# Moving the substitution rounds of a DeltaNet layer behind weight splits and the scaling of the last keys

## The chip, the cores and the metric

The kernel runs on one core of a Trainium2 chip, as one launch. The metric is the device time of an execution in microseconds (us); less is better. The core has five engines, each with an instruction queue of its own that is worked off in order: TensorE (PE in the profile; its weight loads are PEld), VectorE (DVE), ScalarE (ACT), GpSimd (POOL), and SyncE (SP), which here only issues transfers. ScalarE also issues some transfers of weights.

## The reference

One layer of a hybrid diffusion backbone, on 1024 latent tokens and 256 context tokens, width 1024, all in float32. A normalised and modulated input goes through one projection into two branches:

```python
h = rmsnorm(x, g_pre) * (1.0 + scale[:, None]) + shift[:, None]
na_q, na_k, na_v, na_z, g_qkv, g_z, g_b, g_a = jnp.split(h @ w_in, IN_SPLITS, axis=-1)
o_na = neighborhood_attention(...)            # 8 heads of 64, 8 x 16 window on a 16 x 64 grid, plus context keys
q, k, v = gdn_qkv(g_qkv, conv_w)              # 5-tap conv, SiLU, l2norm of q and k; 4 heads of 128
q, k = axial_rope(q, rope), axial_rope(k, rope)
beta, g = gdn_gates(g_b, g_a, A_log, dt_bias)
o_g, o_gc = bidirectional_gdn(q, k, v, g, beta, qc, kc, vc, gc, betac)
o_g = rmsnorm(o_g, gdn_norm_w)
y = jnp.concatenate([o_na * jax.nn.silu(na_z), o_g * jax.nn.silu(g_z)], axis=-1) @ w_out
x = x + gate[:, None] * rmsnorm(y, g_post)
```

The second branch is a gated delta rule in chunks, in both directions. Each chunk needs the inverse of a unit triangular matrix (`triangular_solve`), and `l2norm` divides queries and keys by the root of a sum of squares.

## The kernel before

Products are made from two halves: each operand is split into a high half (`hi`, rounded on ScalarE) and a low half (`lo`, the rest), and three matmuls (hi hi, hi lo, lo hi) add up in PSUM, so each weight goes through L585 (high half, ScalarE) and L586 (low half, GpSimd or VectorE) in `load_w` before TensorE can use it. The raw weights have three buffers; the transfer of a later weight, issued on ScalarE's queue (L582), waits until a raw buffer has been split.

Phase 0 normalises and modulates the inputs. Phase 2 runs over the four DeltaNet heads h. For each head, a string of letters gives the order in which the steps are emitted: Q, K, V (`conv`: projection and convolution), R (`res_gate`), T (`qk_tok`), B (`qk_back`), U (the values' transposes), p (the next part of `projections`, work for TensorE from the attention branch and the gates), and F (`delta_front`, the products of the head's keys and queries, emitted once the next head's Q and K are). In the last head the p's are a key projection of the attention (`na_proj`), the two halves of a gate (`gate_proj`, L704 its last instruction on VectorE), and the first two tiles of `values`, for which the weight `nv0` is loaded in four pieces (k0 = 0, 2, 4, 6; `wr_nv`, `wh_nv` and `wl_nv` in the profile).

`qk_tok` transposes queries (`which` = 1) and keys (`which` = 0) to token order, takes the sums of squares on ScalarE (L1068), takes the keys' root on GpSimd (`rsqrt`, L218 and L219), scales the keys by it on VectorE (L1074) and rotates both: L1084 and L1085 are the products with sine and cosine, L1086 the sum. The queries' rotation is on GpSimd, the keys' on VectorE, and both share two buffers `rot` (tag `sr`). The queries are not scaled here; their roots (`rho`, L218 and L219 on 32 columns) are taken in `delta_load` and used in the scan. `qk_back` transposes back (L1097, `tb`) and stores. `delta_front` follows with `pk` (PE), `pm` and `qe` (VectorE, L1189 and L1192), stores them, and copies `pm` from memory to memory (L1200, `ab_dram`).

`inv_pairs` inverts the 32 x 32 diagonal blocks of the first heads, two groups of 120 blocks side by side, one block a partition, in 30 substitution rounds from m = 30 down to 1; a round is a product (L1233) and a sum (L1235) on VectorE over 2 m (31 - m) elements. It starts in the last head: it yields after the load and after every even m, and the loop over the letters advances it by one yield per letter. At its end the blocks are stored (L1241, `yd`). In phase a2, which runs the rest of the projections (`na_proj` of pairs 2 and 3 among them), `inv_merge` loads the blocks (L1285, `vl`), transposes them on VectorE (L1291 to L1293, `vx`, `vd`, `ld`) and merges them into the chunk's inverse with small products (L1305 the first, `tz`). Then come attention and scan together (phase b) and the output projection (phase 4).

The order of each engine's queue is fixed when the kernel is built, by a list scheduler that keeps a time line of its own estimates: of what is ready there, it takes what was emitted first (`tc.high_priority` lets the merges count as emitted earlier). `self.order(r, name)` adds to it that instruction r stands behind another one; for two instructions of one engine this is an order on the queue and no wait.

Of the kernel before, what the change touches and what calls it, by code (L numbers as in the profile page):

```python
# [11 lines left out]
F32 = mybir.dt.float32  # L12
# [8 lines left out]
P = 128  # L21
# [110 lines left out]
def bc(ap, shape):  # L132
    return ap.to_broadcast(shape)
# [57 lines left out]
class K:  # L191
# [21 lines left out]
            self.nc.sync.dma_start(self.dbg[name], ap)  # L213


    def rsqrt(self, pool, x, n, tag, eps):
        y = pool.tile([P, n], F32, name=f"rq_y_{tag}", tag=f"rq_y{n}")
        self.nc.gpsimd.tensor_scalar(y, x, eps, None, ALU.add)  # L218
        self.nc.gpsimd.tensor_tensor(y, y, bc(self.mhalf, [P, n]), ALU.pow)  # L219
        return y  # L220


# [347 lines left out]
    def load_w(self, pool, c0, n, tag, bufs=(3, 4, 4), halves=2, load=None, ks=None, dst=None, later=None):  # L570


        nc = self.nc
        kk = len(ks) if ks else KC // halves
        his, los = [], []
        for k0 in [ks[0]] if ks else range(0, KC, kk):
            wt = lambda c, dt, nb: pool.tile([P, 528], dt, name=f"w{c}_{tag}_{k0}", tag=f"w{c}", bufs=nb)[
                :, :kk * n].rearrange("p (k n) -> p k n", k=kk)
            raw = wt("r", F32, bufs[0])
            hi, lo = dst or (wt("h", F32R, bufs[1]), wt("l", F32R, bufs[2]))  # L580
            src = self.I["w_in"]
            (load or nc.scalar.dma_start)(raw.rearrange("p k n -> p (k n)"), bass.AP(  # L582
                src.tensor, W_OFF[tuple(c0) if isinstance(c0, list) else ((c0, n),)] + k0 * n, [[KC * n, P], [1, kk * n]]))
            if later is None:
                nc.scalar.copy(hi, raw)  # L585
                (nc.vector if halves > 2 and k0 % 4 else nc.gpsimd).tensor_tensor(lo, raw, hi.bitcast(F32), ALU.subtract)  # L586
            else:
                later.append(lambda c, hi=hi, lo=lo, raw=raw: nc.scalar.copy(hi, raw) if c == "h" else
                             nc.vector.tensor_tensor(lo, raw, hi.bitcast(F32), ALU.subtract))
            for j in range(kk):  # L590
                his.append(hi[:, j, :])
                los.append(lo[:, j, :])
        return his, los
# [102 lines left out]
    def gate_proj(self, ap, ps, j, c0, w=None):  # L696
        nc = self.nc
        w = w or self.load_w(self.wp, c0, P, f"gz{j}")
        for gr in range(2):
            pz = ps.tile([P, 512], F32, name=f"pz{j}_{gr}", tag="pj", bufs=3)  # L700
            self.mm_chan(pz, w, self.hh, self.hl, 512 * gr, 512)
            z = self.wp.tile([P, 512], F32, name=f"st_z{j}{gr}", tag="st", bufs=4)
            nc.scalar.activation(z, pz, AF.Tanh, scale=0.5)
            nc.vector.scalar_tensor_tensor(z, z, 1.0, pz, ALU.add, ALU.mult)  # L704
            nc.sync.dma_start(self.z_dram[P * j:P * j + P, 512 * gr:512 * gr + 512], z)
            yield

# [239 lines left out]
    def phase2(self):  # L947
        tc, nc, I = self.tc, self.nc, self.I
        ps = self.ps
        with tc.tile_pool(name="cv", bufs=1, side="right", reuse_waits="tile") as cv:  # L950
# [37 lines left out]
            for h in range(4):  # L988
                for c in "QK":
                    step(h, c)  # L990
                    next(blocks, None)
                for _ in blocks:
                    pass
                step(h - 1, "F") if h else step(h, "G")
                if h == 3:
                    blocks = self.inv_pairs(cv)
                for c in ("RVpppTUpB", "RppVTpUBp", "RVTpUpB", "VRppTppUB")[h]:
                    step(h, c)
                    next(blocks, None)
            step(3, "F")  # L1000
            for _ in blocks:
                pass
# [47 lines left out]

    def qk_tok(self, cv, ps, h, qa, ka, rope):
        nc, col = self.nc, self.col
        toks = []
        for which, acc in ((1, qa), (0, ka)):
            groups = ((2, 4), (6, 4)) if which else ((0, 2), (2, 4), (6, 4))
            first, m = groups[0][0], 10 - 2 * which
# [2 lines left out]
            for t0, n in groups:  # L1059
# [9 lines left out]
                                         accum_out=ss[:, t0 + t - first:t0 + t - first + 1])  # L1069
                pts.append((t0, n, pt, tok))  # L1070
            r = None if which else self.rsqrt(cv, ss, m, f"g{h}", 4 * EPS)
            for t0, n, pt, tok in pts:
                if not which:
                    nc.vector.tensor_tensor(tok[:, :n, :], pt[:, :n, :],  # L1074
                                            bc(r[:, t0 - first:t0 - first + n].unsqueeze(2), [P, n, P]), ALU.mult)
                if t0:
                    rot = cv.tile([P, 4, P], F32, name=f"rot{h}_{which}{t0}", tag="sr", bufs=2)
                    x5, r5 = (v.rearrange("p t (a s c) -> p (t a) s c", a=2, s=2) for v in (tok, rot))

                    xs = bass.AP(tok.tensor, tok[:, 0, 32:].offset, [list(tok.ap[0]), [64, 8], [-32, 2], [1, 32]])  # L1080
                    cs = rope[:, 64 * (t0 - 2):64 * (t0 + 2)].rearrange("p (b c) -> p b c", c=32)
                    sn = rope[:, 512 + P * (t0 - 2):512 + P * (t0 + 2)].rearrange("p (b s c) -> p b s c", s=2, c=32)
                    eng = nc.gpsimd if which else nc.vector
                    eng.tensor_tensor(r5, xs, sn, ALU.mult)  # L1084
                    eng.tensor_tensor(x5, x5, bc(cs.unsqueeze(2), [P, 8, 2, 32]), ALU.mult)  # L1085
                    eng.tensor_tensor(tok, tok, rot, ALU.add)  # L1086
                toks.append((which, t0, n, tok))
        return toks

# [130 lines left out]
    def inv_pairs(self, pool):  # L1220
        nc = self.nc
        ab = pool.tile([P, 2 * S], F32, name="ab", tag="ab")
        tb = pool.tile([P, 480], F32, name="tb", tag="tb")[:120]
        for g in range(2):
            w = self.inv_load(g, ab[:, S * g:S * g + S])
            nc.gpsimd.affine_select(w, w, [[-1, 32], [1, 32]], ALU.is_gt, 0.0, base=0, channel_multiplier=0)
        ab = ab[:120].rearrange("p (g a b) -> p g a b", g=2, a=32)
        nc.gpsimd.memset(bass.AP(ab.tensor, ab.offset, [list(ab.ap[0]), [S, 2], [33, 32]]), 1.0)
        yield
        for m in range(30, 0, -1):  # L1230
            n = 31 - m
            t3 = tb[:, :2 * m * n].rearrange("p (g a b) -> p g a b", g=2, a=m)
            nc.vector.tensor_tensor(t3, bc(ab[:, :, 0:m, m:m + 1], [120, 2, m, n]), bc(ab[:, :, m:m + 1, m + 1:], [120, 2, m, n]),  # L1233
                                    ALU.mult)
            nc.vector.tensor_tensor(ab[:, :, 0:m, m + 1:], ab[:, :, 0:m, m + 1:], t3, ALU.add)  # L1235
            if m % 2 == 0:
                yield
        yield
        for g in range(2):
            self.yd[g] = self.dp.tile([120, 32, 32], F32, name=f"yd{g}")  # L1240
            nc.sync.dma_start(self.yd[g], ab[:, g])  # L1241
# [112 lines left out]
    def delta_load(self, g3, h):  # L1354
# [10 lines left out]
        if h == 0:  # L1365
# [1 line left out]
            nc.vector.tensor_scalar(fl(self.nsc), fl(self.egc), -1.0, None, ALU.mult)  # L1367
            nc.vector.tensor_tensor(self.nsc[:, :, 1, :], self.nsc[:, :, 1, :], self.beta[:, :, 1, :], ALU.mult)

            self.rho = self.rsqrt(self.cp, self.ssq.rearrange("p h t -> p (h t)"), 32, "rho", 4 * EPS)  # L1370
            self.rho2 = self.cp.tile([P, 32], F32, name="rho2")
            nc.gpsimd.tensor_tensor(self.rho2, self.rho, self.rho, ALU.mult)
        return kq, v, kt_, *(w.rearrange("p (d t) c -> p d t c", d=2) for w in (tm, qe))
# [390 lines left out]
```

## Time and profile before

| what | value |
|---|---|
| time, median of 3 runs | 853.98 us (848.8 to 854.83) |
| the profiled execution's own time | 848.82 us |
| its span, first to last instruction | 847.1 us |
| TensorE busy | 814.2 us, 96% |
| VectorE, ScalarE, GpSimd busy | 495.0, 418.0, 365.5 us |
| granted TensorE clock, mean | 0.99 |

Lines of a timeline give start, duration, engine, source line, operation, output and input, count, and in brackets the idle time of the engine before it with what ended it. Lines of waits give who waited for whom, the total, the number of times and the longest. L586 is line 586 of the kernel before.

### The profile page before, as it was taken

Reading aid. Unit: us, or ns where it says so; the run is one execution under the profiler, and the core shown is the slowest. Engines: PE = TensorE matmul, PEld = TensorE weight load, DVE = VectorE, ACT = ScalarE, POOL = GpSimd, SP = SyncE. Lnnn points to the kernel's source line nnn. Section 1 sums busy time; section 2 is a strip of 40 time slices with the busy share of each in tenths; the row PEclk is TensorE's granted clock in tenths of the full one; section 3 lists DMA queues with packets and bytes.
Section 4 is the critical chain, followed back from the end, with each engine's and each line's share of the span. In section 5 each row is a group of like instructions: output and inputs, shape, how many; then the busy total and the mean of one; then the engine's idle time right before and its main releaser. Section 6 shows DMA issues by size and latency. Waiting matters only on the chain.

```text
span 847.1 us, 16613 instructions
## 1 busy us (share of the span) xinstructions
PE 814.2 (96%) x6170; PEld 695.3 (82%) x6170; DVE 495.0 (58%) x988; ACT 418.0 (49%) x1097; POOL 365.5 (43%) x436
## 2 busy tenths in 40 slices
PE   8999999999999999988997999899999999999996
PEld 6688887888788878878985787799898989878885
DVE  4673455546456757699926955556566565743342
ACT  4472525654564664643214334566666666753211
POOL 0042221363482572555452103565757567835121
PEclk9999999999999999999998999999999999999999
DMA  9986442254626626733688579996967923234261
GB/s 332 341 305 213 136 138 90 79 180 161 162 75 227 197 69 230 218 110 102 202 241 239 166 223 293 392 306 181 313 186 257 250 97 128 87 125 137 99 199 50
DMA packets 86343, 159.67 MB, mean 188 GB/s; under 512 B 18405, under 2 KB 45750, under 8 KB 84086
## 3 DMA queue, kind: packets, MB, share of 16 engines
q1 hardware_dynamic: 78774, 144.94, 54.0%
q10 hardware_dynamic: 7488, 13.67, 5.5%
q8 instruction: 49, 0.80, 0.4%
q14 instruction: 32, 0.26, 0.1%
HBM read 109.51 MB, written 52.42 MB: 191 GB/s over the span
## 4 chain that ended last, share of the span: by engine, by line
PE 76%; DMA 9%; DVE 7%; POOL 3%; issue 2%; ACT 2%; SPq 0%; DVEq 0%; POOLq 0%; ACTq 0%
PE py L1550 4%; PE py L1552 3%; PE py L1551 3%; PE pz L607 3%; PE pz L608 3%; PE pz L603 3%; PE pa L1437 3%; DMA vl<-yd 2%; PE po L942 2%; PE po L937 2%; PE tr L926 2%; PE sc L905 2%; PE pa L1422 2%; PE pv L618 2%; PE pv L617 2%; PE pv L616 2%
## 5 line engine op out<-in xcount | busy, mean ns | idle before, releaser
L909 DVE CUSTOM_DVE_ANT_0 pt<-sc,gm 128x544 f32<-128x544 f32 (+1 forms) x64 | 49.4, 772 | 32.3 <-PE sc L905 28.6
L910 ACT ACTIVATE pt<-pt,nm 128x544 f32<-128x544 f32 (+1 forms) x64 | 50.5, 789 | 31.1 <-DVE nm L909 30.7
L893 POOL TENSOR_TENSOR gm<-gt,mk 128x288 f32<-128x288 f32 (+1 forms) x48 | 46.5, 972 | 21.8 <-DVE nm L909 18.6
L1412 POOL TENSOR_SCALAR kd<-kt,kd 128x128 f32<-128x128 f32 x72 | 42.7, 604 | 18.7 <-PE pa L1451 18.2
L1040 DVE SCALAR_TENSOR_TENSOR acc_v<-xp_v,cols,acc_v 128x1282 f32<-128x1282 f32 x16 | 33.1, 2068 | 26.9 <-ACT acc_v L1038 26.6
L1193 POOL TENSOR_SCALAR_AFFINE_SELECT qe<-qe 128x256 f32<-128x256 f32 x32 | 29.0, 907 | 39.8 <-DVE qe L1192 39.8
L1616 DVE TENSOR_TENSOR finv<-py,ggb 128x512 f32<-128x512 f32 (+1 forms) x17 | 10.7, 656 | 51.4 <-ACT finv L1615 43.0
L603 PE MATMUL pz<-hh,wh_gz 128*128 128x512 f32 x96 | 38.9, 405 | 0.0
L607 PE MATMUL pz<-hl,wh_gz 128*128 128x512 f32 x96 | 38.8, 405 | 0.0
L608 PE MATMUL pz<-hh,wl_gz 128*128 128x512 f32 x96 | 38.8, 404 | 0.0
L1174 ACT ACTIVATE em<-em,gc 128x128 f32<-128x128 f32 x80 | 25.5, 390 | 25.7 <-DMA em<-gc_dram 22.9
L618 PE MATMUL pv<-wl_nv,hh 128*128 128x264 f32 x104 | 30.5, 296 | 4.8 <-DVE wl_nv L586 4.8
L1189 DVE SCALAR_TENSOR_TENSOR pm<-pk,nsc,em 128x128 f32<-128x128 f32 x80 | 23.5, 342 | 18.5 <-PE pk L1182 14.6
L1418 POOL TENSOR_SCALAR vb<-v,beta 128x128 f32<-128x128 f32 x40 | 24.2, 606 | 23.0 <-DVE y L1424 13.1
L586 POOL TENSOR_TENSOR wl_gz<-wr_gz,wh_gz 128x512 fp32r<-128x512 f32 x12 | 15.5, 1290 | 37.3 <-ACT wh_gz L585 35.8
L926 PE MATMUL tr<-c,pt 128*96 128x128 f32 (+1 forms) x192 | 31.4, 273 | 0.0
L1454 DVE SCALAR_TENSOR_TENSOR s<-s,egl,pa 128x128 f32<-128x128 f32 x64 | 19.4, 342 | 20.1 <-PE pa L1451 20.1
L924 ACT COPY tcx<-tc 128x256 f32<-128x256 f32 x64 | 23.5, 367 | 15.1 <-PE tc L919 14.5
L928 ACT COPY tl<-tr 96x384 f32<-96x384 f32 (+1 forms) x64 | 30.5, 476 | 0.0
L617 PE MATMUL pv<-wh_nv,hl 128*128 128x264 f32 x104 | 30.0, 291 | 0.0
L616 PE MATMUL pv<-wh_nv,hh 128*128 128x264 f32 x104 | 29.2, 292 | 0.0
L1615 ACT ACTIVATE finv<-py 128x512 f32<-128x512 f32 x14 | 8.3, 598 | 38.7 <-PE py L1552 20.5
(469 smaller groups left out, 2859.3 us busy)
## 6 DMA issues: line engine op xcount, KB each, us to landing
wada<-in_w_ada SPq DMA_DIRECT2D x16, 512.0 KB
em<-gc_dram SPq DMA_DIRECT2D x20, 256.0 KB
pm_dram<-pm SPq DMA_DIRECT2D x20, 256.0 KB
tm_dram<-tm SPq DMA_DIRECT2D x8, 640.0 KB
kk<-qk_dram SPq DMA_DIRECT2D x16, 320.0 KB
tm<-tm_dram SPq DMA_DIRECT2D x4, 1280.0 KB
kq_dram<-kq SPq DMA_DIRECT2D x4, 1152.0 KB
kq<-kq_dram SPq DMA_DIRECT2D x4, 1152.0 KB
```

The costliest lines, as they stand in the source:

```text
L603: r = nc.tensor.matmul(ps, wh, xh, start=(k == 0 and first), stop=False)
L607: nc.tensor.matmul(ps, wh, xl, start=False, stop=False)
L608: nc.tensor.matmul(ps, wl, xh, start=False, stop=(k == KC - 1))
L616: nc.tensor.matmul(ps, xh, wh, start=(k == 0), stop=False)
L617: nc.tensor.matmul(ps, xl, wh, start=False, stop=False)
L618: nc.tensor.matmul(ps, xh, wl, start=False, stop=(k == KC - 1))
L893: r = nc.gpsimd.tensor_tensor(self.gm[hh][:, 384 - n:384].rearrange("p (n c r) -> p n c r", c=nco, r=4), gv, self.mk[:, mo:mo + n].rearran ...
L909: nc.vector.tensor_tensor_reduce(pt[:, 384 - n:], sc[:, 512 - n:768], gm[:, 384 - n:], -1.0, 3.0e38, ALU.add, ALU.min, nm)
L910: self.last_exp = nc.scalar.activation(pt[:, 384 - n:], pt[:, 384 - n:], AF.Exp, bias=nm, scale=-1.0, accum_out=sums[:, ct, hh:hh + 1]).in ...
L926: self.pe(nc.tensor.transpose(pl[:m, rc * P:(rc + 1) * P], pt[:, 384 + (rc - 3) * m:384 + (rc - 2) * m], self.ident))
L1412: r = nc.gpsimd.tensor_scalar(kd[d], kt_[:, t, :], self.kd[:, h, d, t:t + 1], None, ALU.mult)
L1550: nc.tensor.matmul(py, mh[:, tt], wh[:, nn], start=(k == W_ORDER[0]), stop=False)
```

## The change

Five edits. In `load_w`, the pieces k0 = 2, 4 and 6 of the four-piece weight have their low half on VectorE, where it was 2 and 6. In the last head, the loop over the letters no longer advances the rounds at letters 3 to 5. Inside the rounds, the product of m = 27 is ordered behind the last low half of `nv0` and behind the last gate product (L704), and the product of m = 26 behind the last scaling of keys (L1074). In `qk_tok` of the last head, the queries' last sums (L1086) are emitted after the keys' root and ordered behind it. The queries' root `rho` is ordered behind the keys' root.

```diff
-    def rsqrt(self, pool, x, n, tag, eps):
+    def rsqrt(self, pool, x, n, tag, eps, after=None):
         y = pool.tile([P, n], F32, name=f"rq_y_{tag}", tag=f"rq_y{n}")
-        self.nc.gpsimd.tensor_scalar(y, x, eps, None, ALU.add)
-        self.nc.gpsimd.tensor_tensor(y, y, bc(self.mhalf, [P, n]), ALU.pow)
+        r = self.nc.gpsimd.tensor_scalar(y, x, eps, None, ALU.add)
+        if after:
+            self.order(r, after)
+        self.last_root = self.nc.gpsimd.tensor_tensor(y, y, bc(self.mhalf, [P, n]), ALU.pow).ins.name
         return y
...
                 nc.scalar.copy(hi, raw)
-                (nc.vector if halves > 2 and k0 % 4 else nc.gpsimd).tensor_tensor(lo, raw, hi.bitcast(F32), ALU.subtract)
+                r = (nc.vector if halves > 2 and k0 else nc.gpsimd).tensor_tensor(lo, raw, hi.bitcast(F32), ALU.subtract)
+                self.split = r.ins.name
...
-            nc.vector.scalar_tensor_tensor(z, z, 1.0, pz, ALU.add, ALU.mult)
+            self.gated = nc.vector.scalar_tensor_tensor(z, z, 1.0, pz, ALU.add, ALU.mult).ins.name
...
-                for c in ("RVpppTUpB", "RppVTpUBp", "RVTpUpB", "VRppTppUB")[h]:
+                for j, c in enumerate(("RVpppTUpB", "RppVTpUBp", "RVTpUpB", "VRppTppUB")[h]):
                     step(h, c)
-                    next(blocks, None)
+                    if j < 3 or j > 5:
+                        next(blocks, None)
...
             r = None if which else self.rsqrt(cv, ss, m, f"g{h}", 4 * EPS)
+            if not which:
+                for tok, rot in late:
+                    self.order(nc.gpsimd.tensor_tensor(tok, tok, rot, ALU.add), self.last_root)
...
-                    nc.vector.tensor_tensor(tok[:, :n, :], pt[:, :n, :],
-                                            bc(r[:, t0 - first:t0 - first + n].unsqueeze(2), [P, n, P]), ALU.mult)
+                    self.scaled = nc.vector.tensor_tensor(tok[:, :n, :], pt[:, :n, :],
+                                            bc(r[:, t0 - first:t0 - first + n].unsqueeze(2), [P, n, P]), ALU.mult).ins.name
...
-                    eng.tensor_tensor(tok, tok, rot, ALU.add)
+                    if which and h == 3:
+                        late.append((tok, rot))
+                    else:
+                        eng.tensor_tensor(tok, tok, rot, ALU.add)
...
+            if m == 26:
+                self.order(r, self.scaled)
+            if m == 27:
+                self.order(r, self.split)
+                self.order(r, self.gated)
...
-            self.rho = self.rsqrt(self.cp, self.ssq.rearrange("p h t -> p (h t)"), 32, "rho", 4 * EPS)
+            self.rho = self.rsqrt(self.cp, self.ssq.rearrange("p h t -> p (h t)"), 32, "rho", 4 * EPS, self.last_root)
```

In the next to last hunk r is the product of round m (L1233).

More of the change, by code (lines that the diff above doesn't have):

```diff
@@ L1052, in qk_tok @@
         nc, col = self.nc, self.col
-        toks = []
+        toks, late = [], []
         for which, acc in ((1, qa), (0, ka)):
@@ L1232, in inv_pairs @@
             t3 = tb[:, :2 * m * n].rearrange("p (g a b) -> p g a b", g=2, a=m)
-            nc.vector.tensor_tensor(t3, bc(ab[:, :, 0:m, m:m + 1], [120, 2, m, n]), bc(ab[:, :, m:m + 1, m + 1:], [120, 2, m, n]),
-                                    ALU.mult)
+            r = nc.vector.tensor_tensor(t3, bc(ab[:, :, 0:m, m:m + 1], [120, 2, m, n]),
+                                        bc(ab[:, :, m:m + 1, m + 1:], [120, 2, m, n]), ALU.mult)
+            if m == 26:
[3 more added lines that the diff above has]
+                self.order(r, self.gated)
             nc.vector.tensor_tensor(ab[:, :, 0:m, m + 1:], ab[:, :, 0:m, m + 1:], t3, ALU.add)
```

## The prediction

> **What bounds the kernel now.** I read the page first, for the busiest engine, and then TensorE's waits, which name the few places where it stops.
>
> ```profile
> PE 814.2 (96%) x6170; PEld 695.3 (82%) x6170; DVE 495.0 (58%) x988; ACT 418.0 (49%) x1097; POOL 365.5 (43%) x436
> ```
>
> ```profile
> PE tz L1305 <- DVE ld L1293: 5.6, 1, 5.6
> PE pv L618 <- DVE wl_nv L586: 4.8, 1, 4.8
> ...
> PE tb L1097 <- DVE tok L1074: 1.9, 1, 1.9
> ```
>
> TensorE (PE) is busy in 96% of the span of 847.1 us, so little but its idle time, 33 us in all, and its slow clock can be won by a change of order. Its two longest waits lie close together: 4.8 us for `wl_nv` (the low half of a values' weight, written by VectorE, DVE) and 5.6 us for `ld` (the inverse blocks, transposed, ahead of the first merge). The next view cuts these stretches out: columns are the stretch, its length, busy time of PE, weight loads, DVE, ACT and POOL, then the granted clock and the DMA share.
>
> ```profile
> 318.90:322.40 3.50, 3.50 (x16) 3.43 (x17) 3.50 (x6) 2.34 (x6) 1.89 (x2) 0.51 0.66 198
> 384.00:387.20 3.20, 2.98 (x13) 2.98 (x14) 3.10 (x7) 2.43 (x14) 3.20 (x1) 0.50 0.50 163
> 447.70:453.30 5.60, 0.04 (x1) 0.00 (x0) 3.48 (x6) 0.85 (x2) 0.00 (x0) 0.89 0.82 202
> 453.30:460.00 6.70, 6.68 (x93) 5.72 (x94) 5.35 (x9) 5.21 (x13) 3.16 (x5) 0.59 0.89 289
> ```
>
> After the first wait PE runs 3.2 us at half clock (0.50): (1 - 0.50) x 2.98 = 1.5 us lost on top of 4.84. **Gap 1 costs 6.3 us.** After the second, 6.7 us at 0.59: (1 - 0.59) x 6.68 = 2.7 us on top of 5.58, so **gap 2 costs 8.3 us**. The first row, after the 1.9 us wait for `tok`, is used further down.
>
> Why is `wl_nv` late? VectorE's timeline (start, duration, instruction) says it:
>
> ```profile
> 375.70 1.38 DVE L1233 TENSOR_TENSOR tb<-ab 120x260 f32<-120x260 f32 x1
> ...
> 382.05 1.45 DVE L1235 TENSOR_TENSOR ab<-ab,tb 120x336 f32<-120x336 f32 x1
> 383.43 0.74 DVE L586 TENSOR_TENSOR wl_nv<-wr_nv,wh_nv 128x528 fp32r<-128x528 f32 x1
> 384.09 0.53 DVE L1233 TENSOR_TENSOR tb<-ab 120x368 f32<-120x368 f32 x1
> 384.54 0.68 DVE L704 SCALAR_TENSOR_TENSOR st_z<-st_z,pz 128x512 f32<-128x512 f32 x1
> ...
> 394.83 1.61 DVE L1074 TENSOR_TENSOR tok<-tp,rq_y_g 128x256 f32<-128x256 f32 x3
> ...
> 426.26 0.22 DVE L1235 TENSOR_TENSOR ab<-ab,tb 120x60 f32<-120x60 f32 x1
> ```
>
> The substitution rounds (L1233 the product, L1235 the sum) stand in the queue ahead of `wl_nv` at 383.43, and they are slow there: 1.45 us for 336 elements, against 0.53 us for 368 just behind. GpSimd (POOL) works on large tiles at that time:
>
> ```profile
> 376.76 1.51 POOL L586 TENSOR_TENSOR wl_nv<-wr_nv,wh_nv 128x528 fp32r<-128x528 f32 x1
> ...
> 380.16 2.98 POOL L1086 TENSOR_TENSOR tok<-tok,rot 128x512 f32<-128x512 f32 x2
> 383.10 5.70 POOL L219 TENSOR_TENSOR rq_y_rho<-rq_y_rho,mhalf 128x32 f32<-128x32 f32 x1
> 388.79 0.24 POOL L218 TENSOR_SCALAR rq_y_g<-ss 128x10 f32<-128x10 f32 x1
> ...
> 389.51 2.45 POOL L219 TENSOR_TENSOR rq_y_g<-rq_y_g,mhalf 128x10 f32<-128x10 f32 x1
> ```
>
> The high half on ScalarE (ACT) had long been there:
>
> ```profile
> 376.69 0.63 ACT L585 CAST wh_nv<-wr_nv 128x528 fp32r<-128x528 f32 x1
> 377.22 0.60 ACT L703 ACTIVATE st_z<-pz 128x512 f32<-128x512 f32 x1
> 378.30 0.33 ACTq L582 DMA_DIRECT2D wr_nq<-in_w_in  x1
> ...
> 384.58 0.28 ACT L1068 ACTIVATE sq<-tp 128x128 f32<-128x128 f32 x1 [5.47 <-DVE wl_nv L586]
> ...
> 386.98 0.28 ACT L1068 ACTIVATE sq<-tp 128x128 f32<-128x128 f32 x1
> ```
>
> `wh_nv` was done at 376.69 + 0.62 = 377.3 (CAST, the copy with rounding); its low half came 6 us later, only because of VectorE's order. ACT then waited 5.47 us for the same `wl_nv` (a weight load, queued ahead of the squares, needs the raw buffer), so the key squares ended at 387.2 and the keys' root ran at 388.79 to 392, behind the 5.70 us root `rho` of the queries.
>
> **The change part by part.**
>
> *Low halves and gate ahead of the rounds.* The product of m = 27 now stands behind the last `wl_nv` and behind the gate's L704. That `wl_nv` can start at 377.3 and end at 378.05. PE's row says when it was wanted:
>
> ```profile
> 384.22 0.59 PE L618 MATMUL pv<-wl_nv,hh 128*128 128x264 f32 x1 [4.84 <-DVE wl_nv L586]
> ```
>
> At 384.22 - 4.84 = 379.4, so gap 1 goes: **-6.3 us** on PE up to that point. One more low half (k0 = 4) moves from POOL, 1.51 us at 376.76, to DVE, some 0.74 us by the row at 383.43; DVE would otherwise wait there for `wh_nv`, so it costs nothing; without that cover it is 0.74 us. All these are orders within one queue, so no new wait for another engine is issued by them.
>
> *The product of m = 26 behind the keys' scaling (L1074).* This one is a hold: every round from m = 26 on queues behind L1074, which waits for the keys' root. After the gate's tanh (377.22 + 0.60 = 377.8) ACT has two issues of weight loads at 0.33 and the eight squares that came late, seven of them between 384.58 and 387.2, 0.40 each: 378.6 with gaps, plus 3.2, is 381.8. The root then takes 0.24 + 2.45 us: 384.5, if POOL is free, which it is, as the queries' sums and `rho` now stand behind the root. So L1074 starts at 384.5 instead of 394.83, and DVE idles from about 379.5 to 384.5. What DVE did after 384:
>
> ```profile
> 384.00:427.00 43.00, 42.78 (x294) 40.52 (x295) 40.61 (x88) 13.47 (x38) 17.62 (x16) 0.96 0.55 172
> ```
>
> Of these 40.61 us, 0.17 (the end of `wl_nv`) and 0.68 (L704) now lie before the hold; the rounds m = 26, 25 and 24, which ran from 375.70 to 383.5, come in behind it. These have 260, 300 and 336 elements in product and sum, 1792 together; without POOL beside them, 1792 x 0.53 / 368 = 2.6 us (they took 7.8). The queries' two sums on POOL (2.98 us at 380.16) now run beside the rounds after the root, which stretches two instructions from 0.5 to 1.45: 1.9 us, between nothing, if the scaling itself lies there, and 2.98, if DVE stands still. So 40.6 - 0.85 + 2.6 + 1.9 = 44.3 us, plus the 43 - 40.61 = 2.4 us that DVE idled: the rounds end at 384.5 + 46.7 = 431.2, or at 427 with no idle and no stretch, against 426.5 now. I take 430, since the front of the last head, on which DVE waited, now comes earlier.
>
> *Where that end decides.* SyncE's queue (start, issue time, transfer) and what it waited for:
>
> ```profile
> 428.75 2.60 SPq L1200 DMA_DIRECT2D ab_dram<-pm_dram  x4
> 431.45 1.15 SPq L1241 DMA_DIRECT2D yd<-ab  x2
> ...
> 439.25 1.86 SPq L1285 DMA_DIRECT2D vl<-yd  x4
> ```
>
> ```profile
> SPq L1200 <- DMA pm_dram<-pm: 4.1, 1, 4.1
> ```
>
> The inverse blocks' store `yd` left only at 431.45, although the rounds ended at 426.5: ahead of it in the queue L1200 waited 4.1 us for the landing of `pm`, work of the last head's front, which follows the keys' scaling. That front moves some 10 us earlier with L1074 (394.83 to 384.5), so L1200 is off the chain and `yd` goes with the rounds' end, 430: 1.5 us earlier. From `yd` to the end of PE's wait for `ld` at 453.3 are 21.9 us, with the load `vl` issued only 7.8 us after the store, on a busy DMA (share 0.82 in the window 447.7 to 453.3); with the front's transfers out of the way I estimate 2.5 us less, a third of those 7.8 (nothing to 5). So `ld` comes about 4 us earlier, PE arrives 6.3 us earlier.
>
> *Small ones.* The keys' rotation on DVE needs the two `sr` buffers which the queries' late sums read: the second is free at about 387.5 (384.5 plus 2.98), the scaling ends at 384.5 + 1.61 = 386.1, so up to 1.4 us of waiting, filled by a round if the queue has one there. The queries' transposes come after the keys' anyway, `rho` is read only in the scan, a later phase: nothing. With `scaled` early the next late thing for PE could be `tb` on `tok`, as in the third head: 1.9 us plus (1 - 0.51) x 3.5 = 1.7 us of half clock, 3.6; it would only eat into the wait at gap 2, so I count nothing.
>
> The Trainium skill, "TensorE: Matmul & The Clock Gate", section "Why this matters for your kernels", asks for no idle gaps over about 3 us; by it such a wait would cost 1.9 us alone. The row at 318.90 does not agree: clock 0.51 behind a wait of 1.9 us.
>
> *The sum.* TensorE's queue is laid down in advance. If it kept its order, gap 2 would grow from 5.6 to 7.9 and 4 us would be left. But the planner (the list scheduler that lays out all queues from its own estimates) sees the rounds held too, and puts the first merge (L1305) behind more of the projections; I take gap 2 at its present size, which leaves gap 1's **6.3 us**. The profiled execution (848.82 us, 847.1 of it the span) would become 842.5; it is the fastest of the runs shown, whose median is 853.98, so I forecast **847.7 us**.
>
> **The rivals.**
> - *`ld` decides alone*: L1305 stays where it is in PE's queue. For it: PE does sit in front of L1305 with nothing else in its queue. Gain 1.5 to 4: 851.
> - *Both gaps close*: the planner puts enough projection work in front of L1305. For it: PE had work of na_proj left after 453.3 (busy 6.68 of 6.70). Against: the rounds end no earlier. 6.3 + 8.3 = 14.6: 839.4.
> - *Slower, the hold is longer*: the squares of the keys stay behind a blocked weight load on ACT, end at 387.2 as now, the root at 389.9, the rounds at 389.9 + 46.7 = 436.6, so `yd` is 5.1 us later than 431.45 and PE waits for it: 859.1. It loses from the point where the root ends after about 387.3 (end of rounds past 431.45 by more than the 2.5 us that I give to the DMA). Against: what blocked the load was the `wl_nv` that now comes first.
> - *POOL's root slows the rounds.* `rho` (5.70 us) runs beside rounds that would take 1.45 instead of 0.5: four instead of eleven, some 3.8 us more, rounds' end 434, 2.5 us behind 431.45, offset by the DMA: 854. The row at 384.09 (0.53 us beside `rho`) speaks against it. The Trainium skill, "GPSIMD Engine Reference", section "Specifications", has contention between GpSimd and any VectorE instruction with two SBUF inputs, which would include these; by that row the trace does not agree for `rho`, though it does for the large sums at 380.16.
> - *The change doesn't do what it says* (the product of m = 27 was behind the low half already): excluded by 382.05 before 383.43.
>
> **How the numbers follow.** Forecast 0.40; `ld` alone 0.23; both close 0.20; longer hold 0.13; `rho` 0.04. Within 1% (8.5 us, about what a measurement of this kernel can tell from no change: the runs shown spread from 848.8 to 854.83) lie the forecast, `ld` alone, `rho`, and half of the longer hold; beyond it on the fast side the closing of both, and a fifth of the forecast (its spread of 3 us reaches 845.4): 0.20 + 0.08 = 0.28. Slower by over 1% is the longer hold's upper half: 0.07. Same: 0.65. The range goes from both gaps closed, 839, to just short of the longer hold, 858.
>
> **What would show it.** Right: no PE wait on `wl_nv` around 380 and no 0.50 clock after it; L1074 of the last head near 385; a DVE idle of 4 to 5 us in front of it, waiting for POOL's `rq_y_g`; rounds of m = 26 to 24 at 0.4 to 0.5 us; L1200 on SyncE well before `yd`. Wrong: `yd` issued after 433; a longer PE wait for `ld` than 8 us; squares on ACT still ending at 387; or a new order past 440 that moves gaps elsewhere, which I cannot see from here.

## The result: no gain, and the profile after

After the change the kernel takes 858.23 us (median of 16 executions, 852.67 to 865.47), before it 850.70 (16 executions, 848.24 to 855.2): ratio 1.0083, 95% interval 1.0061 to 1.0104. I had forecast 847.7, 6.3 us less than the median of the three executions first shown; measured are 7.5 us more than before. The profiled execution of after took 853.74 us, one of its shortest, with a span of 852.0 us and a mean clock of 0.98 (0.99 in that of before).

First the stage that the change aims at, in the timelines of VectorE and GpSimd of after:

```profile
377.52 1.21 DVE L588 TENSOR_TENSOR wl_nv<-wr_nv,wh_nv 128x528 fp32r<-128x528 f32 x1 [1.74 <-ACT wh_nv L587]
378.65 0.67 DVE L707 SCALAR_TENSOR_TENSOR st_z<-st_z,pz 128x512 f32<-128x512 f32 x1
...
384.35 1.62 DVE L1081 TENSOR_TENSOR tok<-tp,rq_y_g 128x256 f32<-128x256 f32 x3 [4.24 <-POOL rq_y_g L221]
```

```profile
382.00 0.25 POOL L218 TENSOR_SCALAR rq_y_g<-ss 128x10 f32<-128x10 f32 x1 [3.84 <-ACT sq L1072]
382.34 1.98 POOL L221 TENSOR_TENSOR rq_y_g<-rq_y_g,mhalf 128x10 f32<-128x10 f32 x1
384.29 2.54 POOL L1078 TENSOR_TENSOR tok<-tok,rot 128x512 f32<-128x512 f32 x2
...
387.37 5.67 POOL L221 TENSOR_TENSOR rq_y_rho<-rq_y_rho,mhalf 128x32 f32<-128x32 f32 x1
```

The last `wl_nv` starts at 377.52 instead of 383.43, the keys' root runs at 382.34, and the scaling starts at 384.35 (forecast: 384.5) behind a wait of 4.24 us. TensorE waits for `wl_nv` no more. SyncE's queue in after:

```profile
412.81 2.60 SPq L1210 DMA_DIRECT2D ab_dram<-pm_dram  x4
435.43 0.79 SPq L1256 DMA_DIRECT2D yd<-ab  x2
440.67 2.50 SPq L1300 DMA_DIRECT2D vl<-yd  x4
```

The copy of `pm` goes at 412.81, off the chain as expected, but `yd` leaves at 435.43, not at 430, and later than the 431.45 of before. TensorE's waits from 390 to 545 us (total, times, longest):

```profile
PE tz L1320 <- DVE ld L1308: 5.4, 1, 5.4
PE pk L606 <- DVE sl_q L682: 1.9, 1, 1.9
PE tu L1359 <- DVE tm L1363: 1.3, 1, 1.3
PE tb L1107 <- DVE tok L1096: 1.2, 1, 1.2
```

Gap 2 has kept its size (5.4 us, 5.6 before), as assumed. New are 1.9 us for `sl_q` (a low half of queries, which VectorE makes between the rounds) and the two below it; a wait of 1.5 us for `tm` at 534 us, which before had, is gone.

Where does the rest go? The scan starts with the first product `pa`, at 541.9 in before and 545.9 in after; to the end of the execution it is then 306.9 and 307.8 us. So nearly all is lost before it. The windows up to that point, before and then after (length, busy PE, weight loads, DVE, ACT, POOL, then the granted clock, DMA share, GB/s):

```profile
310.00:365.00 55.00, 52.92 (x275) 43.59 (x274) 36.08 (x53) 29.41 (x65) 27.80 (x28) 0.97 0.63 191
365.00:390.00 25.00, 19.54 (x121) 17.71 (x120) 24.41 (x32) 12.11 (x47) 18.37 (x14) 0.93 0.24 79
390.00:445.00 55.00, 55.00 (x349) 49.95 (x349) 37.73 (x85) 12.11 (x25) 22.24 (x24) 1.00 0.67 199
445.00:470.00 25.00, 18.98 (x272) 15.15 (x270) 17.36 (x31) 10.89 (x23) 5.75 (x7) 0.86 0.84 242
470.00:515.00 45.00, 44.58 (x700) 36.62 (x698) 34.91 (x74) 19.50 (x43) 6.31 (x10) 1.00 0.68 206
515.00:541.90 26.90, 24.44 (x417) 20.05 (x415) 11.49 (x25) 12.00 (x29) 9.90 (x17) 1.00 0.97 327
```

```profile
310.00:365.00 55.00, 53.01 (x281) 43.27 (x280) 36.47 (x53) 30.59 (x66) 28.06 (x28) 1.00 0.62 192
365.00:390.00 25.00, 23.28 (x166) 21.41 (x164) 16.53 (x28) 13.47 (x51) 16.18 (x12) 1.00 0.36 117
390.00:445.00 55.00, 52.09 (x310) 46.32 (x311) 44.21 (x87) 12.06 (x23) 26.61 (x26) 1.00 0.61 189
445.00:470.00 25.00, 19.61 (x257) 15.73 (x256) 14.88 (x26) 10.09 (x21) 4.43 (x6) 0.80 0.85 221
470.00:515.00 45.00, 43.33 (x689) 36.01 (x688) 35.81 (x78) 16.23 (x35) 4.77 (x6) 1.00 0.64 193
515.00:545.90 30.90, 29.97 (x428) 25.77 (x426) 13.36 (x30) 14.79 (x35) 12.11 (x21) 0.72 1.01 365
```

Each window can be split in three: PE's idle time (length less busy), what the slow clock costs (busy x (1 - clock)), and the rest, the work at full clock. Summed from 310 us to the scan:

| | length | idle | clock | work |
|---|---|---|---|---|
| before | 231.9 | 16.4 | 5.6 | 209.8 |
| after | 235.9 | 14.6 | 12.3 | 209.0 |

The work is the same within 0.8 us, as it should be. From 365 to 390 the idle time falls from 5.46 to 1.72 us and the clock from 1.4 to 0: the gain is there, 5.1 us. Of the idle time 2.9 us come back from 390 to 445, and 8.4 us (0.28 x 29.97) come in as slow clock from 515 to 545.9, the hand-over from the merges to attention and scan, where this execution of before has none. TensorE's timeline of after shows what runs there:

```profile
517.52 0.40 PE L611 MATMUL pz<-hh,wl_gz 128*128 128x512 f32 x1
517.85 1.38 PE L1353 MATMUL tz<-xo,pmf 64*64 64x64 f32 x20
519.42 0.79 PE L1359 MATMUL tu<-tm,z 64*64 64x64 f32 x10 [0.20 <-ACT z L1354]
520.95 1.98 PE L1353 MATMUL tz<-tm,pmf 64*64 64x64 f32 x17 [0.74 <-DVE xo L1344]
...
524.69 1.30 PE L1361 MATMUL tu<-z,xo 64*64 64x64 f32 x10
```

The last projection product is at 517.52. From there to 525.9 only the third head's merge products of 64x64 run; ten of them take 0.79 us at 519.42 and 1.30 at 524.69, the clock having halved between. In before the projections last until 523.8, and the merges stand between them. One difference is in the queue: the first merge product stands behind the 19th of the 24 products of `pz2_0` in before and behind the 18th of `pz2_1` in after, 23 products (of 0.23 us, 5.3 us) later. A reading that suggests itself is that TensorE, free of gap 1, did these 23 while it would have waited anyway, and that they are missing at the end: after 515.1 us, 30 projection products start in before and 11 in after. It is not shown; f2 and f3 below were meant to test it, and e3 speaks against it: in its profile (its slowest execution, 860.6 us) 37 start after 515.1 us, and from 515 us to the scan 10.2 us are lost to the clock all the same.

Why are the rounds late? Timelines of after beside each other, VectorE and GpSimd:

```profile
413.08 1.80 DVE L1243 TENSOR_TENSOR tb<-ab 120x480 f32<-120x480 f32 x1
414.91 1.65 DVE L1250 TENSOR_TENSOR ab<-ab,tb 120x480 f32<-120x480 f32 x1
416.60 0.66 DVE L1243 TENSOR_TENSOR tb<-ab 120x476 f32<-120x476 f32 x1
417.29 1.66 DVE L1250 TENSOR_TENSOR ab<-ab,tb 120x476 f32<-120x476 f32 x1
...
422.98 1.57 DVE L1243 TENSOR_TENSOR tb<-ab 120x420 f32<-120x420 f32 x1
```

```profile
411.57 2.80 POOL L588 TENSOR_TENSOR wl_nq<-wr_nq,wh_nq 128x512 fp32r<-128x512 f32 x2
414.33 1.72 POOL L588 TENSOR_TENSOR wl_nk<-wr_nk,wh_nk 128x512 fp32r<-128x512 f32 x1
417.14 1.29 POOL L588 TENSOR_TENSOR wl_nk<-wr_nk,wh_nk 128x512 fp32r<-128x512 f32 x1 [1.10 <-ACT wh_nk L587]
...
422.45 1.64 POOL L588 TENSOR_TENSOR wl_gz<-wr_gz,wh_gz 128x512 fp32r<-128x512 f32 x1 [4.02 <-ACT wh_gz L587]
```

A round's instruction of 420 to 480 elements takes 0.60 to 0.66 us alone and 1.57 to 1.80 beside a low half on GpSimd. All six low halves of the next projections now run beside rounds. In before the first four did so too (415.7 to 423 us), but only two instructions were stretched there, of 300 elements each, to 1.21 and 1.43 us (0.47 alone); the hold has brought more and longer ones beside them.

### The profile page after: what moved, and what is told of

The parts are those of the page before. It is cut to its first block, busy times and chain, and to the rows that moved or that the text cites. A ratio compares the mean times of both kernels' runs of the same rounds, so it can differ in the third digit from the quotient of the medians.

```text
span 852.0 us, 16618 instructions
## 1 busy us (share of the span) xinstructions
PE 820.1 (96%) x6170; PEld 700.9 (82%) x6170; DVE 493.3 (58%) x989; ACT 418.2 (49%) x1097; POOL 367.6 (43%) x435
## 4 chain that ended last, share of the span: by engine, by line
PE 66%; DVE 14%; DMA 9%; POOL 3%; ACT 3%; issue 3%; SPq 2%; ACTq 0%; DVEq 0%; POOLq 0%
PE py L1565 4%; PE py L1567 3%; PE py L1566 3%; PE pa L1452 2%; PE pz L611 2%; PE pz L606 2%; PE pz L610 2%; PE po L945 2%; PE tr L929 2%; PE sc L908 2%; PE po L940 2%; DVE tb L1243 2%; PE sc L905 2%; PE pa L1437 2%; DVE ab L1250 2%
## 5 line engine op out<-in xcount | busy, mean ns | idle before, releaser
L1199 DVE SCALAR_TENSOR_TENSOR pm<-pk,nsc,em 128x128 f32<-128x128 f32 x80 | 23.6, 342 | 17.5 <-PE pk L1192 13.4
L1329 POOL COPY tm<-ld 32x320 f32<-32x320 f32 x16 | 7.3, 456 | 52.3 <-DMA tm_dram<-tm 24.5
L588 POOL TENSOR_TENSOR wl_gz<-wr_gz,wh_gz 128x512 fp32r<-128x512 f32 x12 | 16.4, 1369 | 29.8 <-ACT wh_gz L587 28.3
```

## The experiments

Executions of one kernel differ in the granted clock, and their time goes with it. Over the 126 executions of before, after and the four parts below, a straight line, time = 1525 - 684 x mean clock, has a correlation of -0.96 (through the 82 of before alone: 1526 - 685 x mean clock, -0.94); I call "at an equal clock" the distance from it. Mean clocks are over all executions of a kernel. Ratios are against before as measured alongside, with medians of 850.2 to 853.1 us.

**Parts of the change.** Three theories: H, the hold of the rounds makes `yd` late and loses the time; P, GpSimd's new order does; C, the clock, as drawn from run to run. e1 takes the hold out of after; e2 puts into before only the low half k0 = 4, the order of m = 27 and the skipped letters; e3 only the edits on GpSimd (keys' root first, late sums, `rho` behind); e4 only the skipped letters and the hold.

```diff
-            if m == 26:                              # e1, from after; e4 adds these two and the letters to before
-                self.order(r, self.scaled)
...
+            if m == 27:                              # e2, to before, with the low half and the letters
+                self.order(r, self.split)
+                self.order(r, self.gated)
...
+                    self.order(nc.gpsimd.tensor_tensor(tok, tok, rot, ALU.add), self.last_root)      # e3, with rho's order
```

> The changed kernel without the order of the product of m = 26 behind the keys' scaling; all else of the change stays. Theory H (the hold on VectorE is what costs: it lets the rounds end 9 us later, and the third head's merges slip behind the last projections, where only small products are left and the clock falls to half): the rounds end near 430, no stretch of over 10 us at half clock between 510 and 550, time 0.990 to 0.997 of before (gap 1 gone, 4 to 8 us). Rival P (GpSimd's new order and the weight splits beside the rounds make them late, not the hold): rounds end at 433 or later and time stays at 1.005 to 1.01. Rival C (it is only the clock that is drawn differently from run to run, whatever the order): the granted clock is about 0.975 here too.

> The kernel before with the low halves' part alone: piece 4 on VectorE, the product of m = 27 behind the last low half and the gate, the rounds not advanced at letters 3 to 5; GpSimd's roots and sums as before. Theory H: the wait of 4.8 us for the low half goes, and time is 0.990 to 0.997 of before, like the run without the hold. Rival P: the same or a little faster than without the hold, since GpSimd is as before. Rival C: 1.005 to 1.01, clock 0.975.

> The kernel before with GpSimd's part alone: the queries' last sums and their root stand behind the keys' root. Theory H: the wait for the low half stays (some 4 us), time 0.995 to 1.003 of before. Rival P: 1.005 or more. Rival C: 1.005 to 1.01 with a clock of 0.975.

> The kernel before with the hold alone: the product of m = 26 behind the scaling of the last keys, the rounds not advanced at letters 3 to 5; low halves and roots as before. Theory H: the low half is no longer behind the rounds m = 26 to 24, so the wait for it shrinks, but the root still comes behind the queries' root, near 389, so that the rounds end past 435, the merges bunch up behind the projections, and time is 1.005 to 1.015 of before with a clock near 0.975. Rival P: as before or faster (0.995 to 1.002). Rival C: no difference to the other three.

| | median us | ratio (95%) | mean clock | at an equal clock | `yd` |
|---|---|---|---|---|---|
| before | 851.7 | | 0.985 | +0.1 | 431.5 |
| after | 858.2 | 1.0083 (1.0061 to 1.0104) | 0.975 | +0.2 | 435.4 |
| e1 | 859.7 | 1.011 (1.0046 to 1.0174) | 0.9735 | +0.5 | 428.7 |
| e2 | 856.7 | 1.0051 (1.0011 to 1.009) | 0.977 | -1.0 | 426.8 |
| e3 | 855.9 | 1.0066 (1.0032 to 1.0101) | 0.977 | -0.1 | 430.0 |
| e4 | 862.9 | 1.0142 (1.0069 to 1.0214) | 0.969 | +0.2 | 440.2 |

H falls, though e4 came out in its range: without the hold `yd` leaves 6.7 us earlier and the kernel is no faster. So does P as the only cause: e2 leaves GpSimd's order as it was and loses too. At an equal clock all take the time of before within about 1 us; what differs is the clock, which is lower in each of them. It isn't chance alone, since five new orders, though they share edits, all came out lower. That led to theory S: TensorE needs a supply of full-size products (128x512) at the hand-over.

**Supply and order.** f1 emits one more group of 24 gate products at the end of the projections; f2 is before with its first merge product ordered behind the 18th of `pz2_1`, as in after; f3 is after with the later projections ordered behind the first head's first merge products (`tz1` the last of them), near where they stand in before. `tz0` is the first merge product; `hook` and `behind` add the order at one product of the group.

```diff
+        pz = self.ps.tile([P, 512], F32, name="pz_more", tag="pj", bufs=3)      # f1
+        self.mm_chan(pz, self.last_w, self.hh, self.hl, 512, 512)
...
+                         hook=(lambda n: self.order(self.tz0, n)) if (j, gr) == (2, 1) else None)      # f2
...
+            self.mm_chan(pz, w, self.hh, self.hl, 512 * gr, 512, behind=self.tz1 if (j, gr) == (2, 0) else None)      # f3
```

> After, with one useless group of 24 gate products (128x512, 0.23 us apart, 5.5 us in all) at the end of the projections; its result is not read. It is pure extra work, so by its length alone the time is 858.2 + 5.5 = 863.7 us. Theory S (dense supply): after's 10 us come from the hand-over near 515 to 560 us, where the third head's merge products (32x32 and 64x64) find too few 128x512 products to stand between, and the granted clock halves. Then the extra group mends it: less than 8 us at half clock there instead of 17, mean clock .982 or more instead of .975, time 853 to 857, ratio to before 1.001 to 1.006, faster than after despite the extra work. Theory C (the clock is drawn by chance or set by the whole program): clock .975, time 862 to 865, ratio 1.012 to 1.017.

> Before, with its first merge product ordered behind 23 more projection products, where it stands in after; nothing else of the change. Theory S: TensorE's wait for ld falls from 5.6 us to 1 or less, and the 5.3 us saved are lost with more at the hand-over, where these products are now missing: mean clock .974 to .979, time 855 to 859, ratio 1.005 to 1.010. Theory C: the wait is filled and nothing else moves: time 846 to 851, ratio .995 to 1.000, clock as before (.985).

> After, with its first merge product held in front of the 23 projection products, where it stands in before; the rest of the change stays. Theory S: TensorE waits 10 to 11 us for ld instead of 5.4, the 23 products stand later, the half clock at the hand-over shortens, mean clock .982 to .986, time 849 to 854, ratio .999 to 1.004: a longer wait makes it faster than after. Theory C: the longer wait is paid in full: 863, ratio 1.013 to 1.017, clock .975 or less.

f1: 861.1 us, 1.0112 (1.0039 to 1.0185), clock 0.983: the clock came back as S says, the time did not; at an equal clock it is 8.4 us slower, more than the 5.5 us of products. f2: 863.0, 1.0141 (1.0066 to 1.0216), clock 0.977 as S says, but not a clean trial: on TensorE a wait of 7.4 us for `sl_k`, which stands on VectorE's queue behind the transposes that wait for `vl`, took the place of the wait for `ld`, and at the hand-over came one of 3.2 us for a transfer of keys (`kk<-qk_dram`), during which the clock fell. In f2's timeline of VectorE:

```profile
451.29 1.25 DVE L1294 STREAM_TRANSPOSE vx<-vl 128x1024 f32<-128x1024 f32 x1 [5.69 <-DMA vl<-yd]
...
457.68 0.68 DVE L679 TENSOR_TENSOR sl_k<-pk,sh_k 128x512 fp32r<-128x512 f32 x1
```

f3: 862.3, 1.0124 (1.0061 to 1.0187), clock 0.9775: S missed. The wait for `ld` grew to 9.0 us as meant, and the projections lasted to 524.8 us, but it isn't a clean trial either: at the hand-over TensorE waited 2.95 us for the keys' transfer, and the clock halved at 533.4 us, just behind it. In f3's timeline of TensorE:

```profile
532.90 0.36 PE L911 MATMUL sc<-kk,qh 128*128 128x256 f32 x1 [2.95 <-DMA kk<-qk_dram]
```

The order of one product doesn't bring the clock back.

**The stretch of the rounds.** f4 uses the high half in place of the low one for six weight pieces, g4 puts the six subtractions on VectorE.

```diff
+                if tag in ("nq2", "nk2", "gz2"):        # f4
+                    lo = hi
...
-                r = (nc.vector if halves > 2 and k0 else nc.gpsimd).tensor_tensor(
+                r = (nc.vector if halves > 2 and k0 or tag in ("nq2", "nk2", "gz2") else nc.gpsimd).tensor_tensor(      # g4
```

> After, with GpSimd's six low-half subtractions of the weights nq2, nk2 and gz2 left out: the high half stands in for the low one, so these products are computed from other numbers, at the same size and order. It tests the step on the rounds' end. If GpSimd's large two-input work stretches the rounds beside it (the 7 us by which they ended late), the store of yd starts at 428 to 431.5 instead of 435.4, TensorE's wait for ld falls from 5.4 to under 2 us, and the half clock behind it goes. If it is something else (the gates and scaled low halves among the rounds), yd stays at 434 to 436. The time: with the order unchanged the hand-over keeps its half clock, so 852 to 856, ratio 1.000 to 1.005 by theory S; by the forecast's own sum 847.7 or less, ratio under .996.

> After, with the six low-half subtractions of nq2, nk2 and gz2 on VectorE instead of GpSimd, nothing left out. If GpSimd's subtractions stretch the rounds by 6.6 us (f4's store of yd at 428.8 against 435.4), six of 0.65 to 0.75 us on VectorE itself cost 4.2: yd at 432 to 434, TensorE's wait for ld 3 to 4 us instead of 5.4, and with the hand-over as in after (clock .975) 855 to 858 us, ratio 1.004 to 1.008. If the stretch is something else, yd comes later than 437 and the time is 859 to 862.

SyncE and VectorE of f4:

```profile
428.78 0.79 SPq L1259 DMA_DIRECT2D yd<-ab  x2
```

```profile
411.09 0.66 DVE L1246 TENSOR_TENSOR tb<-ab 120x480 f32<-120x480 f32 x1
411.78 0.66 DVE L1253 TENSOR_TENSOR ab<-ab,tb 120x480 f32<-120x480 f32 x1
412.48 0.66 DVE L1246 TENSOR_TENSOR tb<-ab 120x476 f32<-120x476 f32 x1
```

Without the six, the instructions of 480 elements take 0.66 us, and `yd` leaves at 428.78: the stretch is worth 6.6 us of the rounds' end, and without it they end near the forecast's 430. The wait for `ld` is gone from the list, the kernel takes 852.1 us, 1.0011 (0.997 to 1.0051), and is 5.1 us faster than before at an equal clock; but the clock is 0.977, and the hand-over at 0.56, so nothing shows against before. g4: `yd` at 432.84 as expected, a wait for `ld` of 1.7 us (expected: 3 to 4), 856.3 us, 1.0039 (1.0 to 1.0077), clock 0.978; at an equal clock -0.4. Its profile, the fastest of its executions (850.21 us), has a wait of 4.8 us for the keys' transfer at the hand-over.

**Does the slow clock cost the time, or only go with it?** g1 (after), g3 (before) and g5 (g4) set 12 useless products of 128x128 by 192 columns between the merges of the third and fourth heads; h1 (before, 4 in the fourth head), h2 (e2, 8) and h3 (after, 8) shorter ones of 96 columns.

```diff
             nc.scalar.copy(z2[B, d, t0:t0 + n], pz[B, :n])
+            if h == 2:
+                nc.tensor.matmul(pz[:, 5:, :], self.ident, self.c128[:, :192], start=True, stop=True)
```

> After, with 12 useless full-size products (128x128 by 192 columns, f32, into unused columns of the same PSUM tiles) set between the merge products of the third and fourth heads, where f1 had added a group of projections ahead of them. Theory S, narrowed after f3: the clock halves where 64x64 and 32x32 products follow one another for some 3 us with nothing of full size between them. Then the half clock at 515 to 560 us falls from 17 us to 6 or less, mean clock .982 or more; the 12 cost at most 0.4 us each, 4.8 in all by f32 128-column rows of 0.3 to 0.4 us, and what of it falls into waits is free: 852 to 857 us, ratio 1.000 to 1.006. If size and density of the products are not it: clock .975, 860 to 863, ratio 1.010 to 1.014.

> Before, with the same 12 useless products; about half of before's executions show the half clock at the hand-over too (those at .975 to .984). Theory S: these go, mean clock .987 or more in every run, time 848 to 852, ratio .997 to 1.001 with a smaller spread. Otherwise: clock spread as before, 853 to 856, ratio 1.002 to 1.006.

> After with both: the six subtractions on VectorE, and the 12 full-size products between the merges of the third and fourth heads. Theory S with the stretch: the two add up, yd at 432 to 434, clock .982 or more, time 849 to 854, ratio .997 to 1.003. Without theory S: clock .975, 858 to 862, ratio 1.007 to 1.012.

> Before, with 4 short useless full-size products (128x128 by 96 columns, f32), two each in the two small-tile steps of the fourth head's merges; g3's 12 of 192 columns held the clock in all its executions but showed two records of 0.3 to 0.4 us each, so they took about 8 us of TensorE. These 4 take about 4 x 0.33 = 1.3 us. If the half clock at the hand-over is what makes before's slower executions slow (cause), mean clock .988 or more and 847 to 850 us, ratio .994 to .999, spread smaller. If the half clock only goes with them (no cause): 852 to 854, ratio 1.001 to 1.003.

> The low halves alone (e2), with 8 such short products: four in the last steps of the third head's merges and four in the fourth head's; 2.6 us of TensorE. If the half clock is the cause: mean clock .984 or more instead of .977, 850 to 853 us, ratio .998 to 1.002, under e2's 1.005. If not: clock as may be, 858 to 860, ratio 1.007 to 1.010.

> After, with the same 8 short products. Cause: mean clock .982 or more instead of .975, 853 to 856 us, ratio 1.000 to 1.005, under after's 1.008. No cause: 860 to 862, ratio 1.010 to 1.013.

| | median us | ratio (95%) | mean clock | without the products |
|---|---|---|---|---|
| g1 | 862.7 | 1.0111 (1.0057 to 1.0165) | 0.982 | after 0.975 |
| g3 | 853.2 | 1.0008 (0.9982 to 1.0033) | 0.988 | before 0.985 |
| g5 | 860.0 | 1.0105 (1.0064 to 1.0146) | 0.981 | g4 0.978 |
| h1 | 850.6 | 1.0011 (0.9965 to 1.0058) | 0.987 | before 0.985 |
| h2 | 854.3 | 1.0041 (0.9993 to 1.0088) | 0.985 | e2 0.977 |
| h3 | 862.5 | 1.0135 (1.0085 to 1.0185) | 0.973 | after 0.975 |

The long products raise the clock (in g3 all ten executions are at 0.985 or more, in before they go down to 0.974), but cost as much as they bring or more: some 7 us of work in g1 and g3 by the sum of the windows, not 4.8. The widest difference of two profiles is that of e2 and h2, the window up to the scan:

```profile
515.00:547.60 32.60, 31.41 (x397) 26.53 (x395) 11.85 (x26) 15.07 (x36) 10.40 (x18) 0.60 0.98 357
```

```profile
515.00:540.60 25.60, 24.33 (x418) 20.32 (x416) 11.53 (x27) 14.92 (x36) 10.72 (x18) 1.00 0.95 327
```

With eight more products in it the stretch is 7.0 us shorter, at 1.00 instead of 0.60. But the two are not alike: h2's profile is its fastest execution (848.76 us at 0.990; the other five 853.8 to 859.3 at 0.978 to 0.986), e2's an ordinary one. In the medians 2.4 us are left (856.7 to 854.3), within what the intervals allow to be nothing. In h3 the same products left the clock where it was. Of the times, that of g3 came out just above the theory's range (its ratio within), those of h1 and h2 between the theory and its rival, those of g1, g5 and h3 in the rival's range or just above.

So that a slow clock costs time is seen in the products themselves (0.79 and 1.30 us for the same ten) and in the executions of one kernel, before's 82, where order and work are the same. That filling the hand-over wins the time back is not shown by any of these runs.

**Was gap 1 on the path?** At an equal clock after gains nothing, though TensorE waits 3.7 us less from 365 to 390. Theory L: time of TensorE ahead of `ld` is off the path. Theory G, the forecast's: it is on it. i1 and i2 add 24 useless products to before, behind the last values' products; i2 holds the first merge product at its place.

```diff
         self.ready.append(True)
+        pz = self.ps.tile([P, 512], F32, name="pz_more", tag="pj", bufs=3)
+        self.mm_chan(pz, [[x[:, :P] for x in c] for c in w], self.hh, self.hl, 0, 512)
         yield from self.na_proj(pool, self.ps, [2, 3])
```

> Before, with a useless group of 24 products (128x512, 5.5 us) right behind the last values' products, near 410 us; nothing else changed, and the order is newly planned: the first merge product comes to stand some 11 products earlier than the added ones push it back, so that more products are left for the end. Theory L (the path runs rounds, ld, four heads of merges, scan; what TensorE does ahead of ld is off it): ld at 452 to 455 as before, scan starts 88 to 92 us later, time 850 to 854, ratio .998 to 1.003. Theory G (the forecast's: time of TensorE ahead of 440 is on the path, a gap of 4.84 us there is worth 4.84 us): 5.5 us more, 856 to 858, ratio 1.005 to 1.009.

> The same, with the first merge product held behind the 19th product of pz2_0, where it stands in before: only the 24 useless products are added ahead of it. Theory L: TensorE's wait for ld falls from 5.6 us to under 1.5, ld itself stays at 452 to 455, and the time too: 848 to 853, ratio .996 to 1.002. Theory G: 856 to 858, ratio 1.005 to 1.009.

i1: 856.3 us, 1.0077 (1.0044 to 1.0109). i2: 861.5, 1.0145 (1.0095 to 1.0195). i1 lies in the range of G, i2 beyond both, so L falls: time added ahead of `ld` costs, 5.9 us for 5.5 us of products in i1. That time taken away there is won in full, they don't show. In i2 the wait for `ld` did vanish, and others came, among TensorE's waits from 390 to 550:

```profile
PE tu L1351 <- DVE tm L1355: 3.4, 2, 3.1
PE tu L1331 <- ACT zt L1316: 3.0, 2, 2.8
```

TensorE bounds this stage as far as the runs show, and the three-way sum, from 310 us to the scan, holds for the other profiles as well (work: 207 to 211 us wherever no product was added):

| | length | idle | clock | work |
|---|---|---|---|---|
| e2 | 237.6 | 12.6 | 16.4 | 208.5 |
| h2 | 230.6 | 11.9 | 5.7 | 213.0 |
| e4 | 245.4 | 14.8 | 23.6 | 207.0 |
| f4 | 235.4 | 9.8 | 17.7 | 207.9 |
| g4 | 233.1 | 17.0 | 6.9 | 209.2 |
| i2 | 240.2 | 14.9 | 10.5 | 214.8 |

In these profiles idle time differs by 7 us, the clock's loss by 18. No kernel here is shown to be faster than before.

## Why the forecast was wrong, step by step

- **Gap 1 goes, 6.3 us.** The mechanism was right: wait and half clock are gone. In the windows it is 5.1 us (3.7 idle, 1.4 clock), and i1 shows that time added there counts.
- **The key squares at 381.8, the root at 384.5, the scaling at 384.5.** Right (381.8, 384.3, 384.35), and with it the rival of the longer hold, by its own condition, is out.
- **The rounds end at 430.** Mis-sized. The sum had 1.9 us of stretch by GpSimd, for the queries' sums alone. It left out the six low halves of the next projections, beside which the moved rounds came to lie: 6.6 us by f4, a smaller part of it hidden in the 40.61 us of before, where four of them stretched two instructions. The views quoted showed the effect (1.45 against 0.53 us); what failed is that I applied it only to the instructions that the diff moves, not to those that the moved rounds come to lie beside.
- **`ld` 4 us earlier, gap 2 at its present size.** `ld` came later (455.6 against 453.3), gap 2 kept its size (5.4). The planner did put the first merge later, as assumed, 23 products.
- **`tb` on `tok` and other small waits at nothing.** There are 2.9 us of idle time from 390 to 445, in waits of 1.9 for `sl_q` and 1.2 for `tok`. This and the 1.3 us more from 470 to 515 take most of the idle time won. The forecast had `tok` only eat into the wait at gap 2; whether that wait would have been longer without these, no run shows.
- **The clock from 515 on had no term.** This is the step that decided. The sum ended at 453 us, and "a new order past 440 that moves gaps elsewhere" stood among the things that would make it wrong, without a price. In the profiles it is 8.4 us; over all executions the mean clock fell from 0.985 to 0.975, and 684 x 0.0099 = 6.8 us is the whole of the loss (means 851.5 and 858.3). That the clock is lost at the hand-over is read from one profile of each kernel; why it fell there stays open.
- **The rivals.** `rho` beside the rounds cost nothing: it ran from 387.37 to 393.0, and two rounds' products there took 0.46 and 0.49 us. The rival that I gave as slower, the longer hold, had the wrong mechanism: that its numbers came near (859.1 us, `yd` 5.1 us later; measured 858.2 and 4.0) is luck. VectorE of after:

```profile
389.24 0.46 DVE L1243 TENSOR_TENSOR tb<-ab 120x300 f32<-120x300 f32 x1
...
391.81 0.49 DVE L1243 TENSOR_TENSOR tb<-ab 120x336 f32<-120x336 f32 x1
```

Not settled is what exactly halves the clock. Missing full-size products are one reading: in after it fell 3.2 us behind the last of them. But in e2 one ends at 520.7 us and the clock fell at 521.3, and before has none of 128x512 from 523.8 us to the scan, only attention's products of up to 128x384 among the small ones, and keeps its clock. Short waits are another: in after, e1 to e4, f2 to f4 and g4 the clock fell during a wait of 0.7 to 4.8 us or within 2.4 us behind it. But before has such a wait and keeps its clock, and in h3 the clock fell at 522.6 us with no wait longer than 0.18 us ahead of it since 515 us, and with products on all 128 rows (`tu<-c`, `tz<-c`) in between. TensorE's timeline of before, then of h3:

```profile
534.47 0.76 PE L1338 MATMUL tz<-tm,pmf 64*64 64x64 f32 x10 [1.54 <-DVE tm L1329]
```

```profile
520.00 0.46 PE L1370 MATMUL tu<-c 128*128 128x96 f32 x2
520.64 0.79 PE L1357 MATMUL tz<-tm,pmf 64*64 64x64 f32 x10 [0.18 <-POOL tm L1331]
521.36 0.46 PE L1359 MATMUL tz<-c 128*128 128x96 f32 x2
...
522.48 0.63 PE L1359 MATMUL tz<-c 128*128 128x96 f32 x2
```

Before itself lies near the edge: its executions go from 0.974 to 0.994. Where the clock falls in the slower of them, no trace shows.

## What to carry to other kernels

Where one engine is the bound, a wait taken away early isn't won until the end of its stage is seen: split the whole stage into idle time, clock loss and work. Here 5.1 us were won near 380 us, and more came back as other waits and a slower clock up to 165 us later. Whether that is because the wait had left full-size products over for a stretch of small ones is not shown. Compare executions at their clock, and look whether the one that was profiled is an ordinary one. And when an order is moved, list what the moved instructions come to lie beside, not only what the diff touches.

## What the runs showed of the hardware that was not expected

- The granted clock of TensorE stood at one half in stretches in which the profile showed it busy nearly throughout, with 64x64 and 32x32 products among its work (e2: 31.41 of 32.60 us busy, mean clock 0.60; after: 29.97 of 30.90, 0.72). The Trainium skill, "TensorE: Matmul & The Clock Gate", section "Why this matters for your kernels", asks for no idle gaps over about 3 us. The traces don't agree: in after the longest wait between 515 us and the fall at 521.1 us is 0.74 us, in h3 0.18.
- GpSimd's subtractions on 128x512 in after stretched VectorE's two-input ones by 0.95 to 1.15 us each (0.66 to 1.80 for 480 elements), the power function on 128x32, 5.67 us long, by nothing that shows (0.46 and 0.49 us for 300 and 336 elements beside it).
